# First tiles loaded in halves on two queues, constants later, and the gated attention's products in halves, in a hybrid attention block

## The chip, the cores and the metric

The kernel runs on one core of one Trainium2 chip. A core has five engines with an instruction stream of their own: TensorE (PE in the profile: matmuls; PEld: the loading of their stationary operand), VectorE (DVE), ScalarE (ACT), GpSimd (POOL) and SyncE (SP). SyncE, ScalarE and GpSimd also start DMA transfers, each on a queue of its own (SPq, ACTq, POOLq); all queues share 16 DMA engines. The metric is the device time of one execution in microseconds (us); lower is better.

## What is computed

One decoder layer over 512 tokens of width 1024, in 32-bit floats, and a final norm:

```
h = rmsnorm(x, norm1_w)
aq, ak, av, bq, bk, bv, br, ba, cq, ck, cv = split(h @ w_in)
y_a = dilated_attention(aq, ak, av)             # 6 heads, three strided windows
y_b = gla(bq, bk, bv, br, ba, ...)              # 4 heads, gated linear attention
y_c = moba_attention(cq, ck, cv)                # 6 heads, block-sparse
x = x + concat(y_a, y_b, y_c) @ w_out
x = x + relu(rmsnorm(x, norm2_w) @ w_ff1)**2 @ w_ff2
return rmsnorm(x, final_norm_w)
```

In `gla` the state follows `S_t = diag(alpha_t) S_(t-1) + k_t^T v_t` and the output is `o_t = q_t S_t`, 4 heads with keys of 32 and values of 64 columns.

## The kernel before

**Precision.** A product of two 32-bit operands is made of three faster ones: each operand is cut into a rounded part (`xh`, `wh`) and a remainder (`xl`, `wl`). ScalarE makes most rounded parts (`ACTIVATE wh<-wraw`), VectorE the remainders (`TENSOR_TENSOR wl<-wraw,wh`). The products are then `xh wh + xl wh + xh wl`. The larger matrix products are also arranged as seven block products in the place of eight.

**The order of instructions.** No loop sets it. Each part of the work is a generator (`fetch`, `cut`, `scaled_x`, `gla` and so on) that yields one instruction at a time, or a list that stays together. `Plan.run` simulates the engines with a cost for each instruction (`Op`, L37 to L82; DMA landings in `Plan.issue`, L132 to L150) and always emits the one that can start first. So the order of each engine's stream is settled when the kernel is built, by these costs. On the chip the engines take their streams in that order and wait for each other by semaphores. `yield ("wait", key)` is a wait inside the planner; on the chip only real dependences between tiles hold an engine back.

**The start.** `start` (L1660) loads the norm weights `nw` on ScalarE's queue and the first x tile on SyncE's, fills small tiles, and lets TensorE multiply a tile of ones `WARM` = 9 times into a bank that nothing reads. `fetch` (L280) then loads on SyncE's queue, in the order of `pieces` (L1648): the weight tile `("0", k)` and the x tile k + 1 in turn, then the weights of the queries and keys and of the values. `cut` and `parts` (L302 to L345) cut each weight tile in its two parts; for the first one VectorE makes the rounded part, columns 0 to 271 and 272 to 527 apart. `scaled_x` (L594) multiplies x tile k by the norm weight and cuts it. `first` (L750) is the first projection: for each of eight k, products into `av` (values of the gated attention, 272 columns), `bq` and `bk`. `load_small` (L621) loads the constants on GpSimd's queue; the planner lets it begin after the second x tile's scaling, but no tile ties it to that on the chip.

**The gated attention.** `gla` (L767) works in blocks of 128 tokens. `levels` (L883) makes scaled keys and queries `kq` for the seven distances 64, 32, ..., 1; `gla` multiplies them into `lp`, two levels at a time, and copies what belongs to the level into `attn[h]` (128 x 4 blocks x 128): on ScalarE piece by piece for levels 64 and 32, on VectorE with a mask (`COPY_PREDICATED`) for the rest (L836 to L841). `carry` makes what passes from block to block (`eq`, `smk`). The output bank `op` (L846 to L859) gathers, for each of four blocks, `eq` times `smk` (not for the first block) and for each head `attn[h]` times the values `vB`.

**After that**, attention of the two other kinds, the output projection (`ops`), and the two layers of the feed-forward part (`f1`, `f2`), whose weights are summed and cut as they come.

In the profile all recorded operations have one line, L133, so tiles' names are used. A 32-bit matmul that is not cut shows as two records.

Of the kernel before, what the change touches and what calls it, by code (L numbers as in the profile page):

```python
# [9 lines left out]
F32 = mybir.dt.float32  # L10
# [16 lines left out]
TAU = 1.0 / 16.0  # L27
LC, LT, LW, LN, WARM = 1.0, 0.5, 1.0, 0.0, 9
SWITCH = 0.2
# [7 lines left out]
class Op:  # L37


    def __init__(self, eng, method, args, kw):  # L40
# [14 lines left out]
        if eng == "tensor":  # L55
            self.mode = inner[-1].shape[0] in (32, 64), args[0].shape[0] in (32, 64)
            wide, long = inner[-1].dtype == F32, max(n, 250) / 2400
            if method != "matmul":
                self.cost = 0.109
            elif wide and inner[-1].shape[0] == 32:  # L60
                self.cost = 0.031
            elif wide:
                self.cost = 0.002 + max(n / 600 / (1 + (args[0].shape[0] == 64)), 0.21)
            elif inner[-1].shape[0] == 64:
                self.cost = max(n / 2260, 0.12) / 2
            else:
                self.cost = 0.0135 + long
        elif eng == "scalar":
            few = sum(a.shape[-1] == 1 and n > 4 for a in inner) + ("accum_out" in kw)
            self.cost = 0.09 + n / 1200 + 0.093 * few  # L70
        elif eng == "vector":
            many = method in ("tensor_scalar", "tensor_copy") and all(a.space == bass.MemoryType.SB for a in inner)
            rate = 0.52 if many else 6.25 if method == "reciprocal" else 1.04
            if method == "tensor_reduce":
                n = 512
            self.cost = 0.075 + n * rate / 1000
        elif eng == "gpsimd":
            self.cost = 0.15 + n * (0.9 if method == "memset" else 2.1) / 1000
# [25 lines left out]
class Plan:  # L104
# [5 lines left out]
    def __init__(self, nc, resources):  # L110
# [6 lines left out]
        self.now = 0.0  # L117
        self.mode = None

    def spawn(self, gen, prio=0):  # L120
# [11 lines left out]
    def issue(self, op, at):  # L132
# [7 lines left out]
        if op.method == "dma_start":  # L140
# [3 lines left out]
            else:  # L144
                self.clock["dge"] = max(self.clock["dge"], t) + 0.47
                self.clock["dma"] = max(self.clock["dma"], self.clock["dge"] + 0.65) + op.size / op.rate
                end = self.clock["dma"] + 2.0
        for n in op.outs:
# [60 lines left out]
@with_exitstack  # L209
def hybrid_block_kernel(ctx: ExitStack, tc: tile.TileContext, xT_d, x_d, w0_d, wv_d, wqk_d, wo_d, w1_d, w2_d,  # L210
                        nw_d, ba_d, wa2_d, gw_d, fw_d, rb_d, oh_d, cst_d, lm_d, out_d):
    nc = tc.nc
# [56 lines left out]
    w0 = []  # L269
# [10 lines left out]
    def fetch():  # L280
        for key, src, n in pieces:
# [16 lines left out]
            raw = raws[key] = big("wraw")  # L298
            yield SP.dma_start(raw[:, :n], src)
            fire(("raw", key))  # L300

    def parts(key, src, n=1024):  # L302
# [14 lines left out]
        if key == ("0", 0):  # L317
            for c in (slice(0, 272), slice(272, n)):
                yield DVE.tensor_copy(hi[:, c], src[:, c])
        else:  # L320
            yield ACT.activation(hi[:, :n], src[:, :n], AF.Copy)
# [9 lines left out]
    def cut():  # L331
        for key, src, n in pieces:
# [9 lines left out]
            yield ("wait", ("raw", key))  # L342
            yield from parts(key, raws.pop(key), n)
            give("raw")
# [249 lines left out]
    def scaled_x(k):  # L594
        yield ("wait", ("x", k))
        for c in (slice(0, 256), slice(256, 512)) if k == 0 else (slice(0, 512),):
            yield ACT.activation(xh[k][:, c], xT[k][:, c], AF.Copy, scale=nw[:, 0, k:k + 1])
        fire(("xh", k))
        if k == 0:
            yield ("wait", ("wh", ("0", 0)))  # L600
        yield DVE.scalar_tensor_tensor(xl[k], xT[k], nw[:, 0, k:k + 1], f32(xh[k]), op0=OP.mult, op1=OP.subtract)
        fire(("xl", k))
# [18 lines left out]
    def load_small():  # L621
        yield ("wait", ("xh", 1))
        for t, d in ((cst, cst_d[:, 0:512]), (smask, cst_d[:, 512:1024]), (hsel, cst_d[:, 1024:1028]), (rb[:34, :12], rb_d),
# [143 lines left out]
    def gla():  # L767
# [43 lines left out]
        for l0 in range(0, len(LEVELS), 2):  # L811
# [17 lines left out]
            for i, (li, L) in enumerate(pair):  # L829
# [3 lines left out]
                for h, r in enumerate(("s", "s", "pt", "pt")):  # L833
                    o4 = attn[h].rearrange("p n (m l) -> p n m l", l=2 * L)[:, :, :, L:]
                    src = lp[h][:, i * 256:i * 256 + 256].rearrange("p (n m l) -> p n m l", n=NB, l=L)
                    if L >= 32:  # L836
                        for j in range(m):
# [11 lines left out]
        for i in range(2):  # L849
            yield ("take", "pt")  # L850
            op_.append(bank("pt", "op"))
        for n in range(NB):
            o = op_[n // 2][:, n % 2 * 256:n % 2 * 256 + 256]
            vb = vB[n // 2][:, n % 2, :]
            if n:
                ops.append(PE.matmul(o, eq[:, n * 128:(n + 1) * 128], smk[n - 1], start=True, stop=False, skip_group_check=True))
            ops.extend(PE.matmul(o[:, h * 64:(h + 1) * 64], attn[h][:, n, :], vb[:, h * 64:(h + 1) * 64],
                                 start=(n == 0 and h == 0), stop=h == 3, skip_group_check=True) for h in range(4))
        yield ops  # L859
# [800 lines left out]
    def start():  # L1660
        yield ACT.dma_start(nw, nw_d)
        yield SP.dma_start(xT[0], xT_d[0])
        fire(("x", 0))
# [4 lines left out]
        for z in (rb, wa2, *oneh, alT):  # L1668
            yield POOL.memset(z, 0.0)
        yield DVE.tensor_scalar(nw2, nw[:, 1], -0.5, None, op0=OP.mult)  # L1670
        yield DVE.tensor_scalar(nnw, nw[:, 0], -1.0, None, op0=OP.mult)
        yield ("take", "mm")
# [98 lines left out]
```

## Time and profile before

| what | us |
|---|---|
| median of three runs | 564.78 (564.45 to 565.18) |
| the profiled execution, its own time | 566.03 |
| its span, from the first to the last instruction | 564.0 |
| TensorE busy | 553.6 (98%) |
| VectorE busy | 479.6 (85%) |
| ScalarE busy | 370.3 (66%) |
| GpSimd busy | 69.0 (12%) |

The spans of matmuls are modelled at their ends, so a busy TensorE is not one at its peak. A row of the timeline gives start, length, engine, line, operation, tiles (written <- read), shape and count; in brackets stands how long the engine had been idle before it, and what released it.

### The profile page before, as it was taken

To read this page: it belongs to the slowest core of one execution; us is meant where nothing else is said; L and a number is where in the kernel's file an instruction comes from. 1 tells how busy PE (TensorE), PEld (TensorE's weight loads), DVE (VectorE), ACT (ScalarE), POOL (GpSimd) and SP (SyncE) were. 2 spreads that over 40 slices of the span, in tenths; PEclk is the share of its full clock that TensorE was granted. 3 is DMA by queue.
4 is the path that set the end of the run, shared out by engine and by line. 5 is a ranking of instruction groups with operands and counts; after the bars stand their busy time and mean duration, and the time that the engine had idled before them with its cause. 6 is when DMAs were issued, how large, how long until landed. Compare 5 with 4: busy or idle time off the path is not lost.

```text
span 564.0 us, 9463 instructions
## 1 busy us (share of the span) xinstructions
PE 553.6 (98%) x3513; PEld 477.8 (85%) x3513; DVE 479.6 (85%) x874; ACT 370.3 (66%) x659; POOL 69.0 (12%) x90
## 2 busy tenths in 40 slices
PE   8999999999999999999999999999999999999995
PEld 7977887786876768899987899988999888999884
DVE  5799899978867988999799995799957799867985
ACT  5755744694865775989766476855477655579553
POOL 5003110000010002110111010120020110011103
PEclk9999999999999999999999999999999999999998
DMA  8945594685134765992989429687378594395803
GB/s 301 400 121 118 91 261 95 205 320 112 37 43 121 254 146 112 268 274 60 278 212 209 158 64 279 198 149 206 113 162 279 121 201 160 94 216 113 150 18 131
DMA packets 29948, 96.58 MB, mean 171 GB/s; under 512 B 3648, under 2 KB 3690, under 8 KB 29904
## 3 DMA queue, kind: packets, MB, share of 16 engines
q0 software_dynamic: 9456, 33.53, 33.4%
q1 hardware_dynamic: 20160, 62.20, 30.9%
q8 instruction: 27, 0.44, 0.3%
q10 hardware_dynamic: 288, 0.27, 0.1%
q14 instruction: 17, 0.14, 0.1%
HBM read 93.86 MB, written 2.13 MB: 170 GB/s over the span
## 4 chain that ended last, share of the span: by engine, by line
PE 83%; DVE 9%; DMA 3%; ACT 2%; issue 2%; SPq 0%; DVEq 0%; ACTq 0%; POOLq 0%
PE f2X L133 14%; PE f1X L133 13%; PE qkps L133 10%; PE f1Z L133 8%; PE f2Z L133 7%; PE ops L133 7%; PE vps L133 5%; PE f1Y L133 4%; PE f2Y L133 3%; DMA wraw<-in_w 3%; PE ptp L133 3%; PE po L133 2%; DVE wl L133 2%; PE sps L133 2%; PE av L133 1%
## 5 line engine op out<-in xcount | busy, mean ns | idle before, releaser
L133 DVE TENSOR_TENSOR wl<-wraw,wh 128x1024 fp32r<-128x1024 f32 (+2 forms) x174 | 192.0, 1110 | 39.5 <-ACT wh L133 39.1
L133 ACT ACTIVATE wh<-wraw 128x1024 fp32r<-128x1024 f32 (+2 forms) x173 | 164.6, 966 | 58.1 <-DMA wraw<-in_w 12.3
L133 PE MATMUL f1X<-yp,wh 128*128 128x256 f32 x512 | 92.7, 283 | 0.0
L133 PEld LDWEIGHTS f1X<-yp,wh 128*128 128x128 f32 x512 | 80.1, 192 | 0.3
L133 POOL DMA_DIRECT2D wraw<-in_w x46 | 40.5, 948 | 270.2 <-DVE wl L133 227.2
L133 PE MATMUL f1X<-yp,wl 128*128 128x256 f32 x256 | 72.5, 283 | 0.0
L133 PE MATMUL f2X<-wh,Al 128*128 128x512 f32 (+1 forms) x132 | 50.6, 383 | 0.0
L133 PE MATMUL f2X<-wh,Ah 128*128 128x512 f32 (+1 forms) x132 | 50.6, 383 | 0.0
L133 PE MATMUL f2X<-wl,Ah 128*128 128x512 f32 (+1 forms) x132 | 50.5, 383 | 0.0
L133 PEld LDWEIGHTS f1X<-yp,wl 128*128 128x128 f32 x256 | 49.1, 192 | 0.1
L133 PE MATMUL f1Z<-yp,wh 128*128 128x256 f32 x256 | 46.3, 283 | 0.0
L133 ACT ACTIVATE h<-h 128x512 f32<-128x512 f32 x56 | 34.7, 625 | 10.5 <-DVE h L133 9.9
L133 PE MATMUL qkps<-xh,wh 128*128 128x512 f32 x96 | 40.1, 418 | 0.0
L133 PEld LDWEIGHTS f1Z<-yp,wh 128*128 128x128 f32 x256 | 39.9, 192 | 0.0
L133 ACT ACTIVATE P<-P,mn 128x512 f32<-128x512 f32 (+3 forms) x48 | 26.5, 555 | 18.8 <-DVE mn L133 18.8
L133 ACT ACTIVATE Ah<-h 128x512 fp32r<-128x512 f32 x40 | 24.0, 620 | 21.5 <-DVE h L133 21.5
L133 PE MATMUL qkps<-xh,wl 128*128 128x512 f32 x96 | 37.6, 392 | 0.0
L133 PE MATMUL qkps<-xl,wh 128*128 128x512 f32 x96 | 37.5, 390 | 0.0
L133 PE MATMUL f1Z<-yp,wl 128*128 128x256 f32 x128 | 36.2, 283 | 0.0
L133 DVE TENSOR_TENSOR Al<-h,Ah 128x512 fp32r<-128x512 f32 x40 | 26.9, 686 | 3.2 <-ACT Ah L133 3.1
L133 PEld LDWEIGHTS f2X<-wl,Ah 128*128 128x128 f32 x132 | 24.8, 188 | 4.9
L133 PEld LDWEIGHTS f2X<-wh,Ah 128*128 128x128 f32 x132 | 24.8, 188 | 4.8
(264 smaller groups left out, 1220.8 us busy)
## 6 DMA issues: line engine op xcount, KB each, us to landing
wraw<-in_w SPq DMA_DIRECT2D x66, 512.0 KB, 5.2
wraw<-in_w POOLq DMA_DIRECT2D x46, 512.0 KB, 6.7
wraw<-in_wqk SPq DMA_DIRECT2D x12, 512.0 KB, 6.0
wraw<-in_wv SPq DMA_DIRECT2D x10, 512.0 KB, 6.7
wraw<-in_wv POOLq DMA_DIRECT2D x8, 512.0 KB, 5.4
wraw<-in_wo SPq DMA_DIRECT2D x8, 512.0 KB, 7.1
wraw<-in_wo POOLq DMA_DIRECT2D x8, 512.0 KB, 5.5
nb<-tab SPq DMA_DIRECT2D x12, 256.0 KB, 3.5
```

Of the source, the lines that this page charges most:

```text
L133: getattr(getattr(self.nc, op.eng), op.method)(*op.args, **op.kw)
```

## The change

The norm weights travel as 16 further columns of the first weight tile's first half (`w0n`); that tile comes in two halves on ScalarE's queue, the first x tile in two halves on SyncE's. VectorE copies the norm weights out of the weight tile. The first tile's remainders are made in halves too. The warm-up goes from 9 to 6 matmuls. `load_small` waits for the third x tile, and a one-element copy on GpSimd that reads this tile makes the chip wait too. In `gla`, level 16 is copied by ScalarE, the products of `eq` come first, and each product of `attn` is made in two halves of 64 output partitions. In the planner the cost of a 32-bit product with 64 output partitions is halved after the lower limit is applied, and DMAs are taken to land 0.5 us after their data, not 2.0, until the first weight tile is under way.

```diff
-LC, LT, LW, LN, WARM = 1.0, 0.5, 1.0, 0.0, 9
+LC, LT, LW, LN, WARM = 1.0, 0.5, 1.0, 0.0, 6
...
-                self.cost = 0.002 + max(n / 600 / (1 + (args[0].shape[0] == 64)), 0.21)
+                self.cost = 0.002 + max(n / 600, 0.21) / (1 + (args[0].shape[0] == 64))
...
+        self.land = 2.0
...
-                end = self.clock["dma"] + 2.0
+                end = self.clock["dma"] + self.land
...
             raw = raws[key] = big("wraw")
-            yield SP.dma_start(raw[:, :n], src)
+            if key == ("0", 0):
+                yield ACT.dma_start(raw[:, :288], w0n_d)
+                yield ACT.dma_start(raw[:, 288:544], w0_d[0][:, 272:528])
+                plan.land = 2.0
+            else:
+                yield SP.dma_start(raw[:, :n], src)
...
         if key == ("0", 0):
-            for c in (slice(0, 272), slice(272, n)):
-                yield DVE.tensor_copy(hi[:, c], src[:, c])
+            halves = (slice(0, 272), slice(0, 272)), (slice(272, 528), slice(288, 544))
+            for c, s in halves:
+                yield DVE.tensor_copy(hi[:, c], src[:, s])
+            fire(("wh", key))
+            for c, s in halves:
+                yield DVE.tensor_tensor(lo[:, c], src[:, s], f32(hi[:, c]), op=OP.subtract)
+            fire(("w", key))
+            return
...
-            yield from parts(key, raws.pop(key), n)
+            raw = raws.pop(key)
+            if key == ("0", 0):
+                yield DVE.tensor_copy(nw, raw[:, 272:288].rearrange("p (c k) -> p c k", c=2))
+                fire("nw")
+            yield from parts(key, raw, n)
+            if key == ("0", 0):
+                yield DVE.tensor_scalar(nw2, nw[:, 1], -0.5, None, op0=OP.mult)
+                yield DVE.tensor_scalar(nnw, nw[:, 0], -1.0, None, op0=OP.mult)
...
         yield ("wait", ("x", k))
+        yield ("wait", "nw")
...
-        yield DVE.scalar_tensor_tensor(xl[k], xT[k], nw[:, 0, k:k + 1], f32(xh[k]), op0=OP.mult, op1=OP.subtract)
+        for c in (slice(0, 256), slice(256, 512)) if k == 0 else (slice(0, 512),):
+            yield DVE.scalar_tensor_tensor(xl[k][:, c], xT[k][:, c], nw[:, 0, k:k + 1], f32(xh[k][:, c]), op0=OP.mult, op1=OP.subtract)
...
     def load_small():
-        yield ("wait", ("xh", 1))
+        yield ("wait", ("xh", 2))
+        yield POOL.tensor_copy(misc[:1, 255:256], xh[2][:1, :1].bitcast(F32))
...
-                    if L >= 32:
+                    if L >= 16:
...
+        for n in range(1, NB):
+            ops.append(PE.matmul(op_[n // 2][:, n % 2 * 256:n % 2 * 256 + 256], eq[:, n * 128:(n + 1) * 128], smk[n - 1],
+                                 start=n < 3, stop=False, skip_group_check=True))
         for n in range(NB):
-            o = op_[n // 2][:, n % 2 * 256:n % 2 * 256 + 256]
-            vb = vB[n // 2][:, n % 2, :]
-            if n:
-                ops.append(PE.matmul(o, eq[:, n * 128:(n + 1) * 128], smk[n - 1], start=True, stop=False, skip_group_check=True))
-            ops.extend(PE.matmul(o[:, h * 64:(h + 1) * 64], attn[h][:, n, :], vb[:, h * 64:(h + 1) * 64],
-                                 start=(n == 0 and h == 0), stop=h == 3, skip_group_check=True) for h in range(4))
+            for h in range(4):
+                for c in (0, 64):
+                    ops.append(PE.matmul(op_[n // 2][c:c + 64, n % 2 * 256 + h * 64:n % 2 * 256 + (h + 1) * 64],
+                                         attn[h][:, n, c:c + 64], vB[n // 2][:, n % 2, h * 64:(h + 1) * 64],
+                                         start=False, stop=h == 3, skip_group_check=True))
...
     def start():
-        yield ACT.dma_start(nw, nw_d)
-        yield SP.dma_start(xT[0], xT_d[0])
+        plan.land = 0.5
+        for i in range(2):
+            yield SP.dma_start(xT[0][:, i * 256:i * 256 + 256], xT_d[0][:, i * 256:i * 256 + 256])
...
-        yield DVE.tensor_scalar(nw2, nw[:, 1], -0.5, None, op0=OP.mult)
-        yield DVE.tensor_scalar(nnw, nw[:, 0], -1.0, None, op0=OP.mult)
```

More of the change, by code (lines that the diff above doesn't have):

```diff
@@ L209, in hybrid_block_kernel @@
 @with_exitstack
-def hybrid_block_kernel(ctx: ExitStack, tc: tile.TileContext, xT_d, x_d, w0_d, wv_d, wqk_d, wo_d, w1_d, w2_d,
-                        nw_d, ba_d, wa2_d, gw_d, fw_d, rb_d, oh_d, cst_d, lm_d, out_d):
+def hybrid_block_kernel(ctx: ExitStack, tc: tile.TileContext, xT_d, x_d, w0n_d, w0_d, wv_d, wqk_d, wo_d, w1_d, w2_d,
+                        ba_d, wa2_d, gw_d, fw_d, rb_d, oh_d, cst_d, lm_d, out_d):
     nc = tc.nc
@@ L1756 @@
     nw = np.stack([n.reshape(8, 128).T for n in (norm1_w, norm2_w)], axis=1)
-    ins = dict(xT=x[0].T.reshape(8, 128, 512), x=x[0], w0=w0, wv=wv, wqk=wqk, wo=wo, w1=w1, w2=w2, nw=nw,
+    ins = dict(xT=x[0].T.reshape(8, 128, 512), x=x[0], w0n=np.concatenate([w0[0][:, :272], nw.reshape(128, 16)], axis=1), w0=w0, wv=wv, wqk=wqk, wo=wo, w1=w1, w2=w2,
                ba=gla_b_a.reshape(128, 1), wa2=gla_w_a2[0], gw=gla_norm_w.reshape(1, 256), fw=final_norm_w.reshape(1, 1024),
```

## The prediction

> **What bounds the kernel now.** I read the busy time of the engines by stretches first, then TensorE's own waits.
>
> ```profile
> core 0: us, PE busy (x) PEld busy (x) DVE busy (x) ACT busy (x) POOL busy (x), PEclk, DMA share, GB/s
> 0.00:10.00 10.00, 7.62 (x41) 6.99 (x42) 3.82 (x11) 4.82 (x8) 7.04 (x19) 1.00 0.82 277
> 10.00:30.00 20.00, 20.00 (x128) 18.17 (x128) 16.60 (x30) 15.58 (x28) 0.07 (x1) 1.00 1.00 375
> 30.00:60.00 30.00, 29.85 (x184) 23.42 (x183) 29.68 (x55) 16.99 (x29) 6.30 (x10) 1.00 0.51 115
> 60.00:85.00 25.00, 25.00 (x227) 20.84 (x226) 23.07 (x51) 15.46 (x28) 3.80 (x5) 1.00 0.79 183
> 85.00:110.00 25.00, 24.51 (x161) 19.64 (x160) 25.00 (x68) 14.09 (x30) 0.00 (x0) 1.00 0.45 120
> 110.00:500.00 390.00, 389.39 (x2445) 337.92 (x2445) 332.27 (x582) 264.26 (x476) 42.22 (x48) 1.00 0.67 174
> 500.00:564.00 64.00, 57.20 (x338) 50.85 (x337) 49.20 (x82) 39.12 (x64) 9.53 (x9) 0.98 0.50 119
> ```
>
> TensorE (PE) is idle for 2.38 us before 10 us and for 6.80 us in the last stretch. Between 10 and 500 us it is idle for 0.15 + 0.49 + 0.61 = 1.25 us in all. So whatever starts TensorE's unbroken stream earlier moves the end by as much, provided that its feeders come along; and an edit that only relieves another engine can win 1.25 us at most. VectorE (DVE) is as full as TensorE from 30 to 60 and from 85 to 110 us.
>
> TensorE's waits (us in total, times, longest), and the chain of work over the first 12 us (start, length, what):
>
> ```profile
> PE av L133 <- ACT wh L133: 1.3, 1, 1.3
> PE ptp L133 <- DVE P L133: 0.3, 1, 0.3
> PE sps L133 <- DVE mn L133: 0.2, 1, 0.2
> ```
>
> ```profile
> 2.10 6.38 DMA wraw<-in_w
> 8.51 0.65 ACT wh L133
> 9.21 0.77 PE av L133 x4
> ```
>
> The one wait worth naming is at 9.21 us: the second weight tile, issued at 2.10, lands at 8.49, ScalarE (ACT) rounds it, and only then can the second step of the first projection run. The timeline says where the first step stood:
>
> ```profile
> 3.81 0.17 DVE L133 TENSOR_SCALAR nw<-nw 128x8 f32<-128x8 f32 x1 [2.79 <-DMA nw<-in_nw]
> 3.81 0.91 ACT L133 ACTIVATE xh<-xT,nw 128x256 fp32r<-128x256 f32 x2 [1.34 <-DMA nw<-in_nw]
> 4.28 0.50 DVE L133 CAST wh<-wraw 128x272 fp32r<-128x272 f32 x2 [0.23 <-DMA wraw<-in_w]
> 4.73 0.73 PE L133 MATMUL av<-wh,xh 128*128 128x272 f32 x4
> 7.25 0.40 PE L133 MATMUL bq<-xh,wl 128*128 128x512 f32 x1
> 7.48 0.40 PE L133 MATMUL bk<-xh,wl 128*128 128x512 f32 x1
> ```
>
> Matmuls of 512 columns follow each other every 0.23 us (7.25, 7.48), so the second step could have started at 7.71. It started 9.21 - 7.71 = **1.50 us** late. That is the prize at the start.
>
> **The change, part by part.**
>
> *Constants later.* The first constant load and the scaling of the third x tile on the timeline, then DMA traffic by queue (packets, MB, share of the engines) from 4.0 to 4.7 us and from 4.7 to 8.5 us:
>
> ```profile
> 2.10 0.74 POOL L133 DMA_DIRECT2D cst<-in_cst  x1
> 9.78 0.73 ACT L133 ACTIVATE xh<-xT,nw 128x512 fp32r<-128x512 f32 x1
> 30.73 0.47 DVE L133 TENSOR_SCALAR diag<-cst,rstd 128x128 f32<-128x128 f32 x2
> ```
>
> ```profile
> q1 hardware_dynamic: 140, 0.26, 100.9%
> ```
>
> ```profile
> q1 hardware_dynamic: 415, 0.77, 57.4%
> q0 software_dynamic: 221, 0.52, 41.8%
> ```
>
> q1 carries SyncE's loads, q0 the constants that GpSimd issues. As q0 starts, q1 falls from 100.9% to 57.4% of the engines. The edit makes GpSimd copy one element of the third x tile first, so its constant loads, at 2.10 now, come after that tile's scaling, at 9.78 or a little earlier. The 0.77 MB that q1 moved in 3.8 us would then take 2.1 us at the rate that it had alone (0.26 MB in 0.7 us), and the second weight tile lands at about 4.7 + 2.1 = 6.8 instead of 8.49 (an estimate). Rounding (0.65) makes 7.45, before 7.71. The cover is 0.26 us; if it is gone, each further us of landing is a us of stall. Bounds: 0 won if it still lands at 8.49, 1.50 if in time. I take 1.50. The constants then collide with weight tiles 4 to 7, which are wanted every 2.98 us (4.73 to 7.71), 0.53 MB each time with the x tile, half of the 1.1 MB that q1 moves alone in that time, so a halved queue just keeps up. The constants are first used at 30.73: no cost. Behind the waiting copy on GpSimd stand only these loads and, long after, the zeroing of the attention tiles.
>
> *First tiles in halves, the norm weight inside the first weight tile.*
>
> ```profile
> xT<-in_xT SPq DMA_DIRECT2D x1, 256.0 KB, 2.9
> nw<-in_nw ACTq DMA_DIRECT2D x1, 8.0 KB, 3.0
> ```
>
> Even 8 KB on ScalarE's queue took 3.0 us, a whole x tile on SyncE's 2.9: halving buys little latency. The first weight half (147 KB) takes the place of that 8 KB load, which landed at 3.81, and is not expected before it; then VectorE must copy the norm weight out before ScalarE may scale x (a new wait; behind it on ScalarE stand all later x scalings). The like operation on 8 columns took 0.17 us. So x would be scaled from about 3.95 instead of 3.81: 0.1 us lost; bounds -0.3 (the half lands at 3.5 and TensorE starts at 4.45) and +0.4 (it lands at 4.2). On SyncE the second half of x takes the place that the first weight tile had, so its third and fourth starts stay the second x and weight tile; ScalarE's second start comes in its idle time before 3.81. The splits of `xl` and `wl` add two VectorE instructions, and two scalings of the norm weight move behind them, in a stretch where it is busy 3.82 of 10 us. Sum of the start: -1.50 + 0.1 = **-1.4 us** (bounds -1.8 and +0.4).
>
> *Three warm-up matmuls fewer.* What they do is seen in weight loads (ns, min/median/max) and in two stretches of the timeline:
>
> ```profile
> L133 PEld LDWEIGHTS warm<-ones x18: 192/333/333, 1.1 to 4.5; 128*128 128x128 f32 x18
> ```
>
> ```profile
> 2.29 1.19 PEld L133 LDWEIGHTS warm<-ones 128*128 128x128 f32 x5
> ...
> 4.42 0.32 PEld L133 LDWEIGHTS warm<-ones 128*128 128x128 f32 x2
> ```
>
> Loads take 333 ns at first, one every (1.19 - 0.33) / 4 = 0.21 us; from 4.42 us on two follow within 0.13 (0.32 - 0.19). So TensorE runs slowly for its first 3.4 us (1.1 to 4.42), though the granted clock shows 1.00. Twelve records (two a matmul) at 0.21 us end near 3.7, and TensorE then idles for 0.8 us inside that time. I cost this at nothing, but it is a rival below. [...]
>
> *Gated attention's products in halves.* Weight loads of the products now, and those of the values' products (`po`), which already write 64 partitions:
>
> ```profile
> L133 PEld LDWEIGHTS op<-vB,attn 128*128 128x128 f32 x32 | 4.2, 191 | 0.2
> ```
>
> ```profile
> 206.74 0.63 PEld L133 LDWEIGHTS po<-th,v 128*64 128x64 f32 x8 [0.35 <-issue]
> ...
> 207.88 0.36 PEld L133 LDWEIGHTS po<-th,v 128*64 128x64 f32 x6 [0.18 <-issue]
> ```
>
> Now 32 records take 4.2 us, 0.131 each, and their 64 columns are fewer than the loads they wait for. After: 64 records of half the load. `po` loads start every (0.63 - 0.14) / 7 = 0.070 us, at densest every (0.36 - 0.14) / 5 = 0.044. So 64 take 2.8 to 4.5 us; in the middle 3.7. A change of array shape shows a 0.35 us gap before `po`; there is one more now, of which matmuls in flight hide about half: +0.2. Sum 3.9 - 4.2 = **-0.3 us**, bounds -1.4 and, if a half costs a whole, 64 x 0.131 + 0.35 - 4.2 = +4.5. I take the middle because `po` is the same shape. [...]
>
> *Level 16 copied by ScalarE.*
>
> ```profile
> 74.95 1.43 DVE L133 COPY_PREDICATED attn<-lmask,lp 128x256 f32<-128x256 int32 x4
> 62.29 1.10 ACT L133 ACTIVATE attn<-lp 32x128 f32<-32x128 f32 x4
> 65.40 0.18 ACT L133 ACTIVATE dg<-ktp 128x16 f32<-128x16 f32 x1
> ```
>
> VectorE loses four copies, 1.4 us. ScalarE gets 4 x 4 = 16 of a quarter of the work, at 0.18 to 0.27 each: 2.9 to 4.4 us. They lie between 60 and 85 us, where ScalarE is idle for 9.5 us and VectorE for 1.9. Behind them on ScalarE wait the roundings of the value weights, on these VectorE, on it TensorE. VectorE's 1.4 us is the late one of the stretch 85 to 110, where TensorE waits 0.49 us. I take **-0.3 us**; bounds -0.5 (all of that idle time) and +1.1 (4.4 - 1.4 less VectorE's slack of 1.9).
>
> *The planner.* The order of instructions comes from its costs; those of short wide products and of the first landings change, so neighbours may swap anywhere. With 1.25 us of idle time in the middle this wins little; I take 0, bounds -0.4 and +0.6.
>
> Sum: -1.4 - 0.3 - 0.3 = -2.0 us. The profiled execution took 566.03 us, its span of 564.0 and 2.03 around it; it becomes 564.0. It is 1.25 us above the median of 564.78, so on the median's footing the forecast is **562.8 us**.
>
> **The rivals.**
>
> *The slow start of TensorE lasts longer.* Idle from 3.7 to 4.5 us, the array may stay slow up to a time T. The first step's 2.98 us of work, begun at 4.6, then ends at T + 2.98 - (T - 4.6) / 2 = 5.28 + T/2, at half speed till T. With one more 3.4 us period, T = 7.9, that is 9.23: the whole prize of the start is gone and 564.78 - 0.6 = 564.2 remains. With two, T = 11.3, it is 10.93, 1.72 late: 564.2 + 1.7 = 565.9, slower. It decides from T = 9.1 on, where the other terms are eaten too (5.28 + 4.55 = 9.21 + 0.6). For it: the warm-up now lasts exactly until the first projection. Against: 2.6 us of the first 3.4 are still busy.
>
> *Given back before 110 us.* VectorE is full from 30 to 60 us. Its run there begins with the row sums:
>
> ```profile
> DVE ss L133 <- PE rsp L133: 3.0, 1, 3.0
> ```
>
> It waits 3.0 us for TensorE there, so an earlier TensorE pulls it along, which speaks against. But x tiles delayed by the moved constants, or ScalarE's 16 copies (+1.1), would stand in the place of the removed wait: -2.0 + 1.4 = -0.6, 564.2.
>
> *It does not do what it says.* The second weight tile lands late for a reason of its own: no 1.50, 564.2 to 564.4.
>
> *A half costs a whole.* The two column halves do not overlap: +4.5 instead of -0.3, so 562.8 + 4.8 = 567.6. It makes the kernel slower once a half record costs more than (4.2 - 0.2 + 1.7) / 64 = 0.089 us; `po` shows 0.044 to 0.070.
>
> **How the numbers follow.** The forecast has 0.60, its own range 561.4 to 563.6. The slow start 0.15 (0.10 of it within 0.2%, 0.05 slower), given back 0.13 (0.12 same, 0.01 slower), not doing what it says 0.05 (same), halves that cost wholes 0.07 (slower). 0.2% is 1.1 us, about what a measurement of this kernel can tell from no change. So faster 0.60, same 0.27, slower 0.13. The range 561.3 to 565.3 leaves out the slower cases and a few hundredths below.
>
> **What would show it.** In the changed profile: no wait of `av` at the second step, and `av` unbroken from about 4.7 us; q0 silent before 9 us; weight loads of 0.19 us from about 4.5 on; products of 64 records in about 3.7 us; TensorE's idle time from 85 to 110 us under 0.49; each later landmark some 2 us earlier, to the end. Wrong it would be if weight loads of 0.33 us reach past 5 us, or idle time appears between 10 and 110 us.

## The result, and the profile after

| | kernel before | changed kernel |
|---|---|---|
| median (lowest to highest) of five runs each, us | 565.18 (564.45 to 565.94) | 569.64 (569.30 to 570.58) |
| ratio to before, 95% interval | | 1.0074 (1.0060 to 1.0087) |
| span of the profiled execution, us | 564.0 | 567.7 |

The change makes the kernel 4.5 us slower. The forecast was 562.8, and its range ended at 565.3. First the busy time by the same stretches as before:

```profile
60.00:85.00 25.00, 24.27 (x176) 19.50 (x172) 21.10 (x47) 21.09 (x49) 4.12 (x5) 1.00 0.72 180
85.00:110.00 25.00, 24.67 (x192) 19.45 (x192) 25.00 (x69) 11.43 (x25) 0.00 (x0) 1.00 0.44 116
110.00:500.00 390.00, 387.50 (x2467) 335.71 (x2467) 333.02 (x585) 263.89 (x476) 42.24 (x48) 1.00 0.65 172
```

TensorE, which had no idle time from 60 to 85 us, now has 0.73; from 110 to 500 us it is idle for 2.50 instead of 0.61. VectorE is busy for 21.10 of the 25 us from 60 to 85 (23.07 before): it was given less work there and also waits more. From 85 to 110 us it is as full as ever. TensorE's waits from 10 to 130 us name the places:

```profile
PE ptp L134 <- DVE oB L134: 1.9, 1, 1.9
PE vps L134 <- ACT dg L134: 0.6, 1, 0.6
PE lp L134 <- DVE attn L134: 0.4, 2, 0.3
```

These sum to 2.9 us, of which before had 0.5. Much of the rest is work that ran slowly. Two places show it. The first is the start (weight loads on the timeline; start, length):

```profile
1.06 2.64 PEld L134 LDWEIGHTS warm<-ones 128*128 128x128 f32 x12 [1.06 <-DVE eps L134]
4.53 0.95 PEld L134 LDWEIGHTS av<-wh,xh 128*128 128x128 f32 x4 [0.84 <-ACT xh L134]
7.37 0.33 PEld L134 LDWEIGHTS bk<-xl,wh 128*128 128x128 f32 x1
8.87 0.19 PEld L134 LDWEIGHTS bq<-xh,wl 128*128 128x128 f32 x1
```

The first projection begins at 4.53, and its loads take 0.33 us until after 7.37. Before, they took 0.19 from 4.42 on. The second place is behind the products (TensorE's matmuls on the timeline):

```profile
110.04 2.08 PE L134 MATMUL op<-vB,attn 128*64 128x64 f32 x64
114.06 0.44 PE L134 MATMUL ptp<-cst,P 128*128 128x128 f32 x2 [1.93 <-DVE oB L134]
114.42 1.50 PE L134 MATMUL sps<-k,q 64*128 64x512 f32 x6
```

and the granted clock there (in the stretches' rows it is the third number from the right):

```profile
112.00:114.00 2.00, 0.12 (x6) 0.00 (x0) 2.00 (x4) 1.40 (x3) 0.00 (x0) 1.00 0.52 88
114.00:116.00 2.00, 1.95 (x9) 1.03 (x10) 1.78 (x3) 0.38 (x1) 0.00 (x0) 0.66 0.91 224
116.00:118.00 2.00, 2.00 (x8) 1.85 (x9) 1.26 (x4) 0.96 (x3) 0.00 (x0) 0.50 1.02 386
```

The 64 halves are quick, but TensorE then waits 1.93 us for VectorE's sum `oB` (a row counts from the modelled end of the last matmul; the gap in the stream is 2.1 us), and behind the wait its clock is at half from 114.6 to 118.0 us (0.66 is the mean of a slice in which it falls).

### The profile page after: what moved, and what is told of

The parts are those of the page before. It is cut to its first block, busy times and chain, and to the rows that moved or that the text cites. A ratio compares the mean times of both kernels' runs of the same rounds, so it can differ in the third digit from the quotient of the medians.

```text
span 567.7 us, 9528 instructions
## 1 busy us (share of the span) xinstructions
PE 555.7 (98%) x3539; PEld 478.8 (84%) x3539; DVE 479.2 (84%) x875; ACT 373.4 (66%) x673; POOL 69.3 (12%) x91
## 4 chain that ended last, share of the span: by engine, by line
PE 82%; DVE 10%; ACT 3%; DMA 2%; issue 2%; ACTq 0%; DVEq 0%; POOLq 0%
PE f2X L134 14%; PE f1X L134 13%; PE qkps L134 10%; PE f1Z L134 8%; PE ops L134 7%; PE f2Z L134 7%; PE f1Y L134 4%; PE vps L134 3%; PE f2Y L134 3%; DVE wl L134 3%; PE ptp L134 3%; PE po L134 2%; PE sps L134 2%; PE av L134 2%; DMA wraw<-in_w 2%
## 5 line engine op out<-in xcount | busy, mean ns | idle before, releaser
L134 DVE TENSOR_TENSOR wl<-wraw,wh 128x1024 fp32r<-128x1024 f32 (+3 forms) x175 | 191.8, 1104 | 38.1 <-ACT wh L134 37.7
L134 PEld LDWEIGHTS f1X<-yp,wh 128*128 128x128 f32 x512 | 80.1, 192 | 0.3
```

Of the source, the lines that this page charges most:

```text
L134: getattr(getattr(self.nc, op.eng), op.method)(*op.args, **op.kw)
```

## The experiments

Every gain or loss below is the difference of two medians taken on the same chip, the kernel before being run beside each group (its median was 564.93 to 565.62). The expectations use letters. O: the planner's new order of instructions is the cause. E: the edits are the cause, in whatever order. C: after the six warm-ups TensorE's clock stays low through the first projection. S: ScalarE's sixteen copies make VectorE late. P: the halves put TensorE ahead, into a wait with a slow clock behind it.

| kernel | median, us | difference to before | ratio, 95% interval |
|---|---|---|---|
| old_order_all | 569.57 | +3.95 | 1.0070 (1.0052 to 1.0088) |
| old_order_start | 565.31 | -0.31 | 0.9995 (0.9984 to 1.0006) |
| old_order_gated | 569.22 | +3.60 | 1.0066 (1.0047 to 1.0084) |
| new_warm9 | 568.18 | +2.56 | 1.0043 (1.0029 to 1.0058) |
| old_order_level16 | 569.43 | +4.23 | 1.0075 (1.0061 to 1.0089) |
| old_order_products | 565.41 | +0.21 | 1.0003 (0.9994 to 1.0012) |
| old_order_best | 564.93 | -0.27 | 0.9993 (0.9984 to 1.0002) |
| old_order_start9 | 564.71 | -0.49 | 0.9989 (0.9981 to 0.9998) |
| level16_in_gaps | 565.26 | +0.21 | 1.0000 (0.9992 to 1.0009) |
| level16_twice | 571.02 | +5.97 | 1.0108 (1.0092 to 1.0124) |
| level16_filled | 567.56 | +2.51 | 1.0046 (1.0034 to 1.0059) |
| new_order_level16_back | 568.59 | +3.54 | 1.0058 (1.0043 to 1.0073) |
| all_in_gaps | 564.63 | -0.30 | 0.9995 (0.9986 to 1.0004) |
| new_order_whole | 567.28 | +2.35 | 1.0043 (1.0030 to 1.0056) |
| new_order_undone | 566.85 | +1.92 | 1.0032 (1.0020 to 1.0045) |
| level16_repeat | 567.58 | +2.65 | 1.0046 (1.0032 to 1.0060) |
| two_on_gpsimd | 563.30 | -1.99 | 0.9963 (0.9949 to 0.9976) |
| two_on_gpsimd_early | 563.74 | -1.55 | 0.9971 (0.9961 to 0.9980) |

### The edits or the order?

The planner orders everything anew for any edit. In the kernels called old_order it still costs and places the old instruction, and other instructions are emitted in its place:

```diff
     def issue(self, op, at):
-        getattr(getattr(self.nc, op.eng), op.method)(*op.args, **op.kw)
+        self.emit(op)
...
+    def emit(self, op):
+        if op.real is None:
+            getattr(getattr(self.nc, op.eng), op.method)(*op.args, **op.kw)
+        else:
+            for x in op.real:
+                x() if callable(x) else self.emit(x)
```

So each edit can be tried alone while every other instruction keeps its place. All edits (old_order_all):

> All edits of the change, but every engine's instructions in the order that the planner gave the kernel before. Theory O (the new planned order is what costs in the middle: the wait before 114 us and the idle times at 67, 84 and 94 us are its own): 563.2 us, that is before's 565.2, less 1.7 for the products, less 0.5 for VectorE's relief, plus 0.2 at the start. Theory E (the edits themselves cost, above all ScalarE's sixteen copies): 568 to 570 us, as the change.

The start's edits, with six warm-ups (old_order_start):

> The start alone (halves, constants later, six warm-up matmuls) in the order of before. Theory C (TensorE's slow time lasts on because it idles after the warm-up): 565.4 us, weight loads of 0.33 us until 8 us or later, the second step of the first projection near 9.4. Without that effect the prize of 1.5 us would show: 563.8.

Level 16 and the products (old_order_gated):

> The gated attention's edits alone (products in halves, level 16 on ScalarE) in the order of before. Theory O: 563.0 to 563.5 us, products of 64 records in 1.9 us. Theory E: 566 us or more, with TensorE idle between 60 and 115 us.

All edits cost 3.95 us in the old order too, so the new order isn't needed for the loss. The start (-0.31) can't be told from nothing. The gated attention's edits bring 3.60 of the 3.95.

### The warm-ups

new_warm9 is the changed kernel in its own order with three more warm-ups:

```diff
         for _ in range(WARM):
             yield PE.matmul(warm[:, :128], ones, ones, start=True, stop=True)
+        for _ in range(3):
+            nc.tensor.matmul(warm[:, :128], ones, ones, start=True, stop=True)
```

> The change with three more warm-up matmuls emitted outside the planner, so nine as before, in the change's own order. Theory C: weight loads of 0.19 us from about 4.5 us, the second step at 7.8 instead of 9.45, and 568.0 us, 1.6 below the change. If the slow time has another cause, 569.6 as the change.

Weight loads in new_warm9:

```profile
3.57 0.93 PEld L1700 LDWEIGHTS warm<-ones 128*128 128x128 f32 x6
4.58 0.70 PEld L134 LDWEIGHTS av<-wh,xh 128*128 128x128 f32 x4
8.68 0.19 PEld L134 LDWEIGHTS bq<-xh,wh 128*128 128x128 f32 x1
```

Three more matmuls that nobody reads make the kernel 1.5 us faster by the medians (1.9 by the differences to before). The loads take 0.19 us from 4.58 on, the second step starts at 8.30 (9.45 in the change; 7.8 was expected, and 0.58 us go into a wait for `xl`), and the first projection begins only 0.05 us later than with six.

In the old order, the start with nine warm-ups (old_order_start9):

> Old places, with the first tiles in halves and the constants later alone; nine warm-ups, products and level 16 as before. Theory C (the six warm-ups ate the gain of the loads): 563.6 to 564.3, second step from about 7.8 us. The rival, that VectorE, which has no gap left from 85 to 110 us, gives the 1.4 us back there: 565.2 to 565.9 with a wait of TensorE for VectorE of about 1.4 us between 75 and 120 us.

In this kernel's profile the second step stands exactly where the prediction put it:

```profile
7.71 0.66 PE L141 MATMUL av<-wh,xh 128*128 128x272 f32 x4
```

Yet by the medians only 0.49 us is won (0.1 to 1.1 by the interval; 564.71 lies between the two ranges expected), not 1.50. The rest isn't lost further on: in this profile TensorE waits only 0.26 us for `mn` at 105 us, and all up to there comes 1.6 us earlier than in the profile before (rows under "A faster kernel"). It is the 1.50 that was one execution's. Where the second step starts differs from execution to execution. Seven other kernels in the old order have the start of before (but read the norm weights out of another tensor). In their profiles it starts at 7.96 to 8.84 us, in the profile before at 9.21. One of them (old_order_products):

```profile
8.11 0.76 PE L141 MATMUL av<-wh,xh 128*128 128x272 f32 x4
```

With the start's edits and nine warm-ups it starts at 7.71 to 8.60 in five profiles. So 9.21 is a late one, and 7.71 an early one: the profile before took 566.03 us, over the median, and that of old_order_start9 563.25, the quickest of its twelve executions.

In the old order three warm-ups fewer can't be told from nothing (-0.31 with six, -0.49 with nine): their price of 1.9 us is measured in the change's own order alone.

### Which of the gated attention's edits?

One of them alone, and everything but level 16 and the six warm-ups:

> The kernel before, every instruction in its old place, with one edit: the sixteen copies of level 16 by ScalarE, the products whole and the start as before. Theory S (these copies are the cause: ScalarE takes its orders in turn, the roundings of weights and e come out later, VectorE waits for them between 60 and 85 us, and is late from 85 to 110, where it has no gap left): VectorE busy 18.9 us of the 25 from 60 to 85 (23.1 before), a wait of TensorE for VectorE between 75 and 120 us, and a time 2 to 4 us over the kernel before: 567.5 to 569.5. Theory P (the cheap halves are the cause: TensorE gets ahead, stands idle and then runs slowly, and the copies alone do little): 565 to 566.3, within 0.2% of the kernel before.

> The kernel before, every instruction in its old place, with one edit: the products in halves of 64 columns, 64 records in some 2 us in place of 32 in 3.7 to 4.2 us. Theory S: VectorE is on time, TensorE keeps most of the 1.7 us: 563.8 to 565, no stretch with a granted clock under 0.95. Theory P: TensorE waits for VectorE by what it gained, and then runs slowly: 566.5 to 569.5, a granted clock under 0.9 behind the wait.

> Old places, with the first tiles in halves, the constants later and the products in halves; nine warm-ups and level 16 on VectorE as before. Theory S: the start gives 1.4 us (weight loads of 0.19 us from the first product on, the second weight tile's products from about 7.8 us) and the products 0.5 to 1.7 us: 562 to 563.5. Theory P: 565.5 to 568, as the products give back what the start wins.

S holds for the loss: level 16 alone costs 4.23 us, as much as all edits together. P holds for the missing gain: the halves alone bring nothing, though at 565.41 they don't cost what P expected either, and old_order_best lies between the ranges of S and P. In old_order_products their block is over in 2.1 us, and TensorE then stands still:

```profile
98.91 2.08 PE L141 MATMUL op<-vB,attn 128*64 128x64 f32 x64
106.02 0.83 PE L141 MATMUL sps<-k,q 64*128 64x256 f32 x6 [1.76 <-DVE mn L141]
107.36 0.63 PE L141 MATMUL vps<-wl,xh 128*128 128x512 f32 x1
```

Before, TensorE waited 0.22 us for `mn`; now it waits 1.76 us. That is 1.5 us more, as much as the halves won: the block with the products of `eq` takes 3.4 us (97.52 to 100.92) where it took 4.9 (98.45 to 103.35).

### How sixteen short copies cost 4 us

ScalarE, VectorE and TensorE on the timeline of old_order_level16, around the place:

```profile
72.00 0.63 ACT L141 ACTIVATE e<-e 128x512 f32<-128x512 f32 x1 [1.45 <-DVE e L141]
72.66 1.82 ACT L141 ACTIVATE attn<-lp 16x64 f32<-16x64 f32 x8
74.50 1.06 ACT L141 ACTIVATE wh<-wraw 128x1024 fp32r<-128x1024 f32 x1
```

```profile
75.59 1.23 DVE L141 TENSOR_TENSOR wl<-wraw,wh 128x1024 fp32r<-128x1024 f32 x1 [1.51 <-ACT wh L141]
76.74 1.41 DVE L141 COPY_PREDICATED attn<-lmask,lp 128x256 f32<-128x256 int32 x4
```

```profile
77.31 3.50 PE L141 MATMUL lp<-kq 32*128 32x64 f32 x64 [0.88 <-DVE attn L141]
81.33 0.63 PE L141 MATMUL vps<-wh,xsl 128*128 128x512 f32 x1
```

In the kernel before, the rounding and the block stood here:

```profile
72.20 1.05 ACT L133 ACTIVATE wh<-wraw 128x1024 fp32r<-128x1024 f32 x1
76.73 2.01 PE L133 MATMUL lp<-kq 32*128 32x64 f32 x64
```

Read it from the top. Eight copies, 1.82 us, stand in ScalarE's queue ahead of the rounding of a weight tile, which so starts at 74.50. Before, it started at 72.20, straight behind `e`. VectorE waits 1.51 us for it. Its next instructions, the copies of level 8, start at 76.74 instead of 74.95. The banks of these copies are those that TensorE's third block of `lp` wants, so TensorE is idle for 0.88 us. Then the block takes 3.50 us instead of 2.01, and 512-column products take 0.63 instead of 0.39. Part of that is the granted clock, which is at half from 79.5 to 86.4 us:

```profile
78.00:80.00 2.00, 2.00 (x56) 1.97 (x58) 2.00 (x7) 0.00 (x0) 0.00 (x0) 0.88 0.91 205
80.00:82.00 2.00, 2.00 (x16) 1.69 (x13) 2.00 (x6) 0.00 (x0) 0.86 (x1) 0.50 0.97 361
86.00:88.00 2.00, 2.00 (x9) 1.64 (x8) 2.00 (x5) 0.23 (x1) 0.75 (x1) 0.91 0.37 33
```

Two experiments test the first step of this chain. level16_in_gaps moves the sixteen copies within ScalarE's queue:

```diff
+            if op.eng == "scalar" and op.outs[0].split("_")[0] in ("e", "wh") and self.holds():
+                self.free16(8)
```

> Old places again, level 16 alone, with ScalarE's sixteen copies in other places of its queue: eight behind the rounding of e that starts at 68.6 us, where ScalarE stood idle for 2.4 us, and eight behind the rounding of a weight tile that starts at 72.2 us, where it stood idle for 2.3 us; VectorE's four copies gone as in the change. Theory S (it is their place in ScalarE's queue, ahead of roundings that VectorE waits for): VectorE's waits for wh and e stay as before, no wait of TensorE at 76 us, 564.3 to 565.6. A rival, that sixteen copies by ScalarE cost what they cost wherever they stand: 567 to 569.5.

level16_twice leaves VectorE its four copies and gives ScalarE sixteen that write elsewhere:

```diff
-o = as_(o, *(ACT.activation(o4[w_, :, j], src[w_, :, j], AF.Copy) for j, w_ in enumerate(cut16)))
+o = as_(o, DVE.copy_predicated(o4, mk, src),
+        *(ACT.activation(scr[w_, :, :], src[w_, :, j], AF.Copy) for j, w_ in enumerate(cut16)))
```

> As old_order_level16, but VectorE also keeps its four copies of level 16, and ScalarE's sixteen go into a tile that nobody reads (so VectorE is relieved of nothing). Theory S says that the loss comes from ScalarE's load in front of the roundings: 569.4 or up to 2 us more. If instead the loss came from what VectorE does or does not do (its order of waits, its four copies missing), it would go: 565 to 566.5.

The same sixteen copies cost 4.23 us in one place of the queue and 0.21, not to be told from nothing, in another. With VectorE not relieved at all they cost 5.97. VectorE's waits from 60 to 85 us in old_order_level16 and in level16_in_gaps:

```profile
DVE kq L141 <- ACT e L141: 3.2, 4, 1.2
DVE wl L141 <- ACT wh L141: 3.2, 2, 1.6
```

```profile
DVE kq L141 <- ACT e L141: 2.4, 3, 1.2
DVE wl L141 <- ACT wh L141: 0.3, 1, 0.3
```

The place in the queue is the cause: the wait for `wh` falls from 3.2 to 0.3 us, which is what the kernel before has.

Two more test the last step, the slow clock. In level16_filled four products with zeros fill TensorE's wait; in level16_repeat they repeat the last real product, so the sum is another one:

```diff
+            acc, _, ww = plan.last.args
+            for _ in range(4):
+                nc.tensor.matmul(acc, zero, ww, start=False, stop=False, skip_group_check=True)
```

> As old_order_level16, with four products of 512 columns with a tile of zeros (0.9 us) put in front of the third block of lp, into a sum that is still open, so that TensorE is not idle while it waits there for VectorE. If the idle time is what takes the granted clock down to 0.5 from 79 to 87 us: the block of lp back at 2.0 us from 3.5, granted clock 1.0, and 565.8 to 566.8, 3 us less. If the clock falls for another reason (the block of small products itself, the load on VectorE), or the lateness is VectorE's own: 568.5 to 570.

> As level16_filled, but the four products that fill the wait repeat the last real one (its tile of weights in place of zeros; the sum is then no longer the reference's). In level16_filled TensorE was never idle there and its granted clock was still 0.5 from 79.5 to 83 us. If products with zeros count as idle: the block of lp at 2.0 us, granted clock 1.0, 565.8 to 566.5. If the 64 small products of lp take the clock down themselves, from where they happen to begin: 567.3 to 568, as with zeros.

Work that does nothing, put into the wait, makes the kernel 1.7 us faster (+2.51 instead of +4.23). So 0.88 us of idle time on TensorE costs more than itself here. But the theory isn't clean: 567.56 lies between the two times expected. TensorE in level16_filled, then in level16_repeat:

```profile
75.60 1.10 PE L860 MATMUL vps<-wl,zero 128*128 128x512 f32 x4
76.64 2.94 PE L141 MATMUL lp<-kq 32*128 32x64 f32 x64
79.92 0.63 PE L141 MATMUL vps<-wh,xsl 128*128 128x512 f32 x1
83.27 0.40 PE L141 MATMUL vps<-wh,xsh 128*128 128x512 f32 x1
```

```profile
76.42 2.94 PE L141 MATMUL lp<-kq 32*128 32x64 f32 x64
79.63 0.40 PE L141 MATMUL vps<-wh,xsl 128*128 128x512 f32 x1
```

With zeros the clock is still low from 79.9 to 83.3 us, half as long as without the filling. With a real product it isn't low at all in this profile. The block takes 2.94 us in both, since VectorE hands over its banks late, one after the other. But the medians of the two, 567.56 and 567.58, don't differ (the spans from the first to the last instruction do: 565.8 and 564.9 by their medians, 563.2 before), and a profile is one execution. Nor do the two profiles differ in the zeros alone: the clock changes of the profiles stand whole steps of 3.413 us behind the place where the weight loads turn quick (shown at the end). 22 steps behind it, the clock falls at 79.8 us in the one (loads quick from some 4.7); in the other this point is at 80.1 (from some 5.05; an estimate). So it stays open whether the small products of `lp` can take the clock down without any idle time. What the two kernels share, some 2.5 us over before, holds the filling (0.9 us) and VectorE's own lateness.

### What happens in the change's own order

Three edits are undone in the changed kernel, every other instruction staying where the change has it: level 16 back on VectorE, the products whole, and both of these with nine warm-ups.

> The changed kernel in its own order with one edit undone: level 16 by four copies on VectorE, each in the place of the last of ScalarE's four. Theory S: the loss between 60 and 100 us (2.9 us in the profile of the change) goes, what was given back at 110 us behind the products stays at least in part: 566 to 567.8. If VectorE's four copies, 1.4 us, make it late in the new order: 569.5 to 571.

> The changed kernel in its own order with one edit undone: the products whole again, 32 records for 64, in the place of the halves. In the change the halves end at 111.9 us, TensorE waits 2.1 us for VectorE's sum and its granted clock is 0.5 from 114.5 to 118 us. If the halves' early end is what takes the clock down there: most of the wait filled by the longer products, granted clock 1.0, and 567.8 to 569 (the clock's 1.5 us less). If the new order or VectorE's lateness does it: 569.6 to 571.5, the products' 1.7 us on top, and the slow clock still there.

> The changed kernel's own order with three edits undone (nine warm-ups, level 16 on VectorE, products whole): what is left of the change is the start's loads, the later constants and the planner's new order. If the sum of the single edits explains the change: 564.5 to 565.7, as the kernel before. If the planner's order costs something by itself: 566 to 568, with a wait of TensorE between 60 and 120 us that the kernel before does not have.

Undone alone, level 16 is worth 0.9 us (4.46 - 3.54; 568.59 lies between the two ranges expected), the halves 2.1 (4.46 - 2.35), the six warm-ups 1.9 (4.46 - 2.56). All three together give only 2.5 (4.46 - 1.92), half of their sum; why, no run shows. With whole products, whose block ends 1.7 us later (113.8 instead of 112.1), TensorE comes to `ptp` at almost the same time and without the slow clock (new_order_whole):

```profile
114.24 0.44 PE L141 MATMUL ptp<-cst,P 128*128 128x128 f32 x2 [0.43 <-DVE oB L141]
114.60 0.96 PE L141 MATMUL sps<-k,q 64*128 64x512 f32 x6
```

`ptp` starts at 114.24 here and at 114.06 in the change: the 1.7 us by which the halves end sooner bring nothing, as the whole block began 0.18 us sooner in the change (108.55 instead of 108.73). Then six `sps` take 0.96 us instead of 1.50. So in the new order the halves make the kernel slower by way of the clock. This isn't only one profile's: the mean granted clock is 0.995 in all five executions of the change and 0.996 to 0.997 in those of new_order_whole, and 3.4 us at half the clock lower the mean by 0.003.

The last 1.92 us belong to the planner's new order (the start's loads, alone, win a little). TensorE's waits from 10 to 130 us in new_order_undone:

```profile
PE vps L141 <- ACT dg L141: 0.6, 1, 0.6
PE ptp L141 <- DVE oB L141: 0.4, 1, 0.4
PE lp L141 <- DVE attn L141: 0.2, 1, 0.2
```

That is 1.2 us, 0.7 more than the 0.5 of before. The rest of the 1.92 isn't pinned to an instruction, nor was it tried which of the planner's changed costs brings the order about.

### A faster kernel

all_in_gaps has every edit in the old order, with nine warm-ups and with level 16 in ScalarE's gaps:

> Old places, first tiles in halves, constants later, nine warm-ups, products in halves, and level 16 by ScalarE in the gaps of its queue as in level16_in_gaps: every edit of the change but the six warm-ups and the planner's new order. If VectorE, relieved of 1.4 us, lets TensorE keep what the start (0.5 us measured) and the products (1.7 us in their block) win: 562 to 563.8. The rival, that TensorE gives the products' 1.7 us back at the wait for VectorE at 107 us, as in old_order_products: 564.2 to 565.2.

The rival holds: 564.63, with the same wait of 1.8 us for `mn`. VectorE's relief of 1.4 us comes at 68 to 73 us, where VectorE had gaps anyway. From 81 us on it has none. two_on_gpsimd takes two instructions out of that stretch instead (level 16 stays on VectorE, as in old_order_best):

```diff
+            if eng == "vector" and op.method == "tensor_tensor" and op.outs[0].split("_")[0] == "wl":
+                self.n_wl = getattr(self, "n_wl", -1) + 1
+                if self.n_wl in (25, 26):
+                    eng = "gpsimd"
```

> old_order_best with two of VectorE's subtractions wl<-wraw,wh (those at 90.2 and 94.0 us, 1.2 us each) done by GpSimd, which did nothing from 85 to 110 us. If VectorE, busy 25.00 of these 25 us, is what takes the products' gain back: the wait of TensorE for VectorE at 107 us falls from 1.8 us to 0.5 or less, and the time from 564.9 to 563 or 563.7. The rival, that a subtraction by GpSimd takes longer than TensorE can wait (its 512 columns took 1.44 us elsewhere, so some 2.9 us for 1024) or slows VectorE: 565 to 567, with a wait of TensorE for POOL wl.

> As two_on_gpsimd, with the subtractions at 86.3 and 94.0 us, so that the two do not follow each other on GpSimd. If in two_on_gpsimd the second one is late behind the first, this one is faster than it by up to 1 us; otherwise the same within 0.3 us.

```profile
PE sps L146 <- DVE mn L146: 0.6, 1, 0.6
```

```profile
85.00:110.00 25.00, 24.07 (x204) 18.59 (x203) 24.17 (x73) 14.53 (x33) 5.11 (x2) 1.00 0.52 151
```

The wait for `mn` falls from 1.8 to 0.6 us, VectorE has idle time there (24.17 of 25), and the kernel takes 563.30 us, 1.99 less than the one before and 6.3 less than the changed one by the medians. The two subtractions take GpSimd 5.11 us. Apart from each other (86.3 and 94.0 us) they do no better, so the second isn't late behind the first. VectorE is the bound from 81 to 107 us, now shown and not only argued from its busy time.

How far such a bound reaches is seen from the row sums `rsp`, for which VectorE waits, to the product that waits for `mn`. The kernel before, old_order_start9, and `rsp` of old_order_products (its `mn` row stands further up):

```profile
24.78 0.95 PE L133 MATMUL rsp<-ones,ssx 128*128 128x2 f32 x8
106.91 0.83 PE L133 MATMUL sps<-k,q 64*128 64x256 f32 x6 [0.22 <-DVE mn L133]
```

```profile
23.17 0.95 PE L141 MATMUL rsp<-ones,ssx 128*128 128x2 f32 x8
105.33 0.83 PE L141 MATMUL sps<-k,q 64*128 64x256 f32 x6 [0.26 <-DVE mn L141]
```

```profile
23.88 0.95 PE L141 MATMUL rsp<-ones,ssx 128*128 128x2 f32 x8
```

The distance is 82.1 to 82.2 us in all three, and in old_order_start, old_order_best and all_in_gaps too. An earlier start moves both ends; the halves, and VectorE's relief at 68 to 73 us, shorten nothing between them. The two subtractions on GpSimd do: 81.0 us in two_on_gpsimd.

## Why the prediction was wrong, step by step

**The start (-1.4).** What it said of the loads came true: the norm weights, copied at 3.77, let TensorE begin at 4.53, the first constant load starts at 8.59 instead of 2.10, and the first projection has no wait for the second weight tile. With nine warm-ups the second step starts at 7.71 in one profile, the foretold place. The size did not come true: the start's edits with nine warm-ups win 0.49 us. The 1.50 was read from one execution, which took 1.25 us more than the median, and was subtracted from the median. Other profiles with the old start have the second step at 7.96 to 8.84, so 0.25 to 1.1 us behind 7.71.

**Three warm-ups fewer (0).** This is the first step that failed: in the change's own order they are worth 1.9 us, by the same matmuls put back. With the idle time of 0.84 us before the first projection TensorE stayed slow until 8.8 us in the change's profile (the load at 8.68 takes 0.26 us, the next one 0.19). That is the rival "The slow start of TensorE lasts longer", with 0.15 of the chance: its formula gives 5.28 + 8.8 / 2 = 9.68, and the second step came at 9.45. The half speed in this formula stands in no row of the prediction; in the change's profile 512-column products start every 0.42 to 0.43 us in the slow time and every 0.23 behind it. The end at 8.8 lies between the two that it reckons with in steps of 3.4 us, 7.9 and 11.3. "2.6 us of the first 3.4 are still busy" was no argument, as no row showed how busy is enough.

**The products (-0.3).** The mechanism was right, the size was not: 64 records take 2.08 us, one every 0.029, instead of 3.7 + 0.2. The rival "A half costs a whole" is refuted. The 0.2 for the change of shape was the author's estimate: in the change the loads stand idle for 0.33 us ahead of the first half (110.04), the matmuls show no idle time there. But the 1.5 us by which the block got shorter were worth nothing in the old order, and the halves cost 2.1 in the new one. The wait that they end in was in no term.

**Level 16 (-0.3).** This step cost most in the old order. The copies took 0.213 to 0.217 us each, within the range given. (The row at 74.95 that the prediction shows is level 8's; the four copies that VectorE lost stood at 68.02 and 71.49 and took 1.5 us.) But the bound of +1.1 set their sum against VectorE's idle sum of 1.9 us and ScalarE's of 9.5 us. What decided was the place: eight of them ahead of a rounding that VectorE wanted at once. The text named the chain ("Behind them on ScalarE wait the roundings of the value weights, on these VectorE, on it TensorE") and priced only its first link. The rival "Given back before 110 us" had the right place with 1.4 us; alone it is 4.23. In the change's own order, level 16 is worth 0.9.

**The planner (0, at most +0.6).** In its new order, with the three edits undone, the kernel is 1.92 us slower, three times the bound; which instruction costs it stays open.

**The frame.** "Whatever starts TensorE's unbroken stream earlier moves the end by as much, provided that its feeders come along": that held for the start, since VectorE waits for TensorE at the row sums (2.98 us before, 3.75 in old_order_start9) and is pulled along. Behind the row sums VectorE, full from 81 to 107 us, doesn't come along. A gain on TensorE between them and 107 us ends in the wait for `mn`; that TensorE waited only 0.49 us there before meant that the two were level, not that TensorE was free to gain. And a low clock behind a wait of TensorE (0.50 from 114.6 to 118.0 us in the change) was in no term after the start. The last sentence of the prediction held: loads of 0.33 us past 5 us, and idle time between 10 and 110 us.

## What to carry to other kernels

When two engines are level, as TensorE and VectorE here from 85 to 110 us (24.51 and 25.00 busy), a gain on one is worth only what the other lets through (the halves' 1.5 us came to nothing): take work out of the full stretch of the second one first (two subtractions moved to an idle engine there won 1.99 us, what no other edit did). To load an engine that "has 9.5 us idle", look at the instruction next behind in its queue and who waits for it; sixteen copies cost 4.2 us or nothing by their place alone. Take the size of a wait from several profiles, or from one whose time is the median. And price a new wait of TensorE at more than its length, or keep TensorE busy through it (0.9 us of products put into a wait of 0.88 us won 1.7 us, level16_filled).

## What the runs showed of the hardware

- A low granted clock followed waits as short as 0.88 us (0.50 from 79.5 to 86.4 us, old_order_level16), but not every wait. Behind the same wait of 1.76 us, 512-column products took 0.63 us in old_order_products and 0.40 in old_order_best:

```profile
106.17 0.83 PE L141 MATMUL sps<-k,q 64*128 64x256 f32 x6 [1.76 <-DVE mn L141]
107.51 0.40 PE L141 MATMUL vps<-wl,xh 128*128 128x512 f32 x1
```

  The times of the clock's changes show what differs. In the trace of the kernel before, the first clock record starts at 4.44 us, and the one change comes 163 times 3.413 us later; in that of the change it starts at 8.81, and the changes come 31, 32 and 163 times 3.413 us later. In both, the weight loads turn quick at that start. In four more profiles the slices' means and the loads give the same steps: the low stretch begins at 113.2 us in new_warm9 (32 steps behind 3.9), 107.4 in old_order_products (30 behind 5.0), 79.5 in old_order_level16 (22 behind 4.4) and 79.8 in level16_filled (22 behind 4.7). It lasts 6.8 us in old_order_level16 and 3.4 in the other three and in the change. Counted so, the wait of old_order_products, 104.26 to 106.02, lies in one step (103.95 to 107.36), at whose end the clock falls; in old_order_best a step ends at about 105.4 (29 behind 6.46, an estimate from its loads), in the middle of the wait. How busy a step must be is not shown.
- At the start the profile's granted clock shows 1.00 (0 to 10 us, before and changed kernel) while weight loads take 0.33 instead of 0.19 us: there the loads' length is the sign to read. Where they turn quick differs between the profiles: at 3.9 to 6.7 us in eleven with nine warm-ups, at 8.8 (the change) and 9.2 (new_order_whole) with six.
- Products with 64 output partitions start every 0.029 us in the change (64 from 110.04 us on in 2.08 us; loads of 0.132 to 0.138), whole ones of the same 64 columns every 0.10 to 0.12 in the kernel before (eight from 98.45 to 99.28, eight from 102.42 to 103.35; both without the products of `eq`).
- GpSimd took 5.11 us for two subtractions of 128x1024 (two_on_gpsimd, 85 to 110 us), some 2.6 each; VectorE took 1.23 for one (at 75.59 us, old_order_level16).
